# Smaller places for raw weights, a tile of their own for Strassen sums, later squares, and eight more Strassen steps in a hybrid decoder block

## The chip, the core and the metric

The kernel runs on one core of one Trainium2 chip. The metric is the device time of one execution in microseconds (us). TensorE multiplies; VectorE (DVE), ScalarE (ACT) and GpSimd (POOL) do the rest; SyncE (SP), ScalarE and GpSimd issue DMAs. Tiles in on-chip memory have 128 partitions; sizes below are bytes per partition unless they are called MB or belong to a DMA.

## The reference

A decoder block on 256 tokens of 4096 channels, all in float32:

```python
h = rmsnorm(x, norm_w[l])
proj = jnp.einsum('bsd,de->bse', h, w_in[l])
u_p, z_p, u_c, b_c, c_c, z_c, g_logit = jnp.split(proj, SPLIT_POINTS, axis=-1)
y_pool = causal_multiscale_pool(u_p, pool_w[l], pool_scale[l]) * jax.nn.silu(z_p)
y_conv = causal_gated_shortconv(u_c, b_c, c_c, conv_w[l], conv_b[l]) * jax.nn.silu(z_c)
ys = jnp.stack([y_pool, y_conv], axis=2)
br = jnp.einsum('bsnc,ncd->bsnd', ys, w_branch[l])
gates = jax.nn.sigmoid(g_logit.reshape(b, s, N_BRANCHES, d) + gate_b[l])
merged = jnp.sum(gates * br, axis=2)
x = x + jnp.einsum('bsd,de->bse', merged, w_out[l])
...
return rmsnorm(x, final_norm_w)
```

Nearly all of the work is in the three matrix products: w_in (4096 x 20480), w_branch (two of 2048 x 4096) and w_out (4096 x 4096).

## The kernel before, in words

**Units and steps.** The output columns are cut into units of 1024. A unit is a list of steps; a step takes 256 rows of the weight matrix, which is a block of 256 x 1024 or 1 MB, loaded as a raw tile of four quarters of 128 x 512 (2 KB each). The units come in the order cz0 cb0 cu0 cc0 cz1 cb1 cu1 cc1 (convolution branch), pz0 pu0 pz1 pu1 (pooling branch), g0_0 to g1_0 (eight gate units), b0_0 to b1_3 (eight branch units of 8 steps) and o0 to o3 (output); all but the branch units have 16 steps of weights. The text of a unit ("PSPSS...", lines 36 to 49) says of what kind each step is. pz1 and g0_0 also hold a step B (the pooling bands) and two steps M (the 512 x 512 maps of the pooling branch).

**A P step** is the plain product: two halves of rows, two of columns, two of tokens. Each float32 operand is split into a rounded part ("high") and the remainder ("low"), and three products high x high, high x low, low x high are summed, so a P step has 2 x 2 x 2 x 3 = 24 matmuls of 128 x 128 by 128 x 512. **An S step** does the same block by Strassen's scheme with seven products in place of eight: 7 x 3 = 21 matmuls. For that it needs sums of weight quarters as well as quarters (`formed` and `plain`), and sums of activations, which stand in the arena or, for activations kept for P steps, in a small `side` tile that a DMA fills.

**Preparing a step.** `highs` (line 241) rounds quarters into cells of the ring with ScalarE; `lows` (line 245) writes raw minus rounded into other cells with VectorE. The ring (line 209) has 26 cells of 2 KB. They are handed out in order, a block only when all of its cells are free; TensorE frees the two cells of a quarter after the products with it. A P step takes 4 + 4 cells. An S step takes blocks of 3, 3, 4 and 4: the rounded first three quarters, their remainders (`whole`), the two outer sums with their remainders (`outer`), the two inner ones (`inner`), in this order. The sums are made in place in the raw tile. The fourth quarter of an S step is first loaded as it is, and then a gather of POOL adds the third quarter to it in memory.

**What sets the order.** The program is written out by one pass over the units. After each product group (`after_group`) the work list is pumped (`pump`, line 1015): a raw load is issued when the step that had its place before is prepared, and the next piece of preparation is issued when it belongs to a step at most four ahead (AHEAD) and its block of cells is free. After every six matmuls (TICK) one entry of a queue is issued, in which the epilogue of the unit before lies: the entry None passes a tick. So each engine has a fixed order of instructions, and an engine that waits keeps back all that stands behind it: ScalarE's roundings, evacuations and squares, VectorE's sums and remainders, POOL's gathers (raw corners, the corner products J added to E, the residual rows), SP's raw loads.

**Places.** `raw` has five places of 8 KB (NRAW). `issue_load` (line 999) loads a P step with one DMA of 1 MB and an S step with one of 256 KB, one of 768 KB and the gather. Place i serves the loads i, i + 5, i + 10 and so on, and is free when the whole step is prepared.

**The epilogue of an output unit** (`out_unit`, line 767) runs during the next unit: POOL adds the corner products J to E with two gathers, then two row gathers add the residual x to E, ScalarE squares the two rows with a running sum (`square`), VectorE multiplies by the final weight, and E is stored to o_d. In the last unit, o3, the residual of the last 1024 columns is loaded into a free raw place (`rest = slot(0)`, line 1195), and the stored rows of the other three units come back into raw places (`unpark`, line 1178), before the final scaling.

Of the kernel before, what the change touches and what calls it, by code (L numbers as in the profile page):

```python
# [15 lines left out]
P = 128  # L16
# [11 lines left out]
NRAW = 5  # L28
# [12 lines left out]
NINE_P = "PSPSSPSPSSPSSPSP"  # L41
# [10 lines left out]
def hybrid_block(ctx: ExitStack, tc: tile.TileContext, x, xc, prm, rows_in, w_in, pool_w, w_branch, w_out, out):  # L52
# [56 lines left out]
    raw = sb("raw", [P, NRAW, 2 * NU])  # L109
# [145 lines left out]
    class Step:  # L255
        def __init__(self, unit, kind, src=None, op=None, **kw):
            self.unit, self.kind, self.src, self.op = unit, kind, src, op
            self.__dict__.update(kw)
            self.raw = None
            self.prepared = self.halved = False  # L260
            self.pre, self.mid = [], []

        def first(self):
# [3 lines left out]
            def rounded(cells):  # L267
                self.q = self.raw.rearrange("p (i c) -> p i c", i=4)
                self.cells = cells
                if self in steps[:2]:  # L270
                    for i in range(4):
                        if self is steps[0] and i == 0:
                            copy(ring[:, cells[0]], self.q[:, 0])
                        else:
                            highs(cells[i:i + 1], self.q[:, i:i + 1])
                elif self.halved:
                    for i in (0, 2):
                        highs(cells[i:i + 2], self.q[:, i:i + 2])
                else:
                    highs(cells, self.q[:, 0:len(cells)])  # L280

            return [(3 if self.kind == "S" else 4, None, rounded)]

        def rest(self):
            if self.kind == "P":
                def rests(to):
                    self.lows = to
                    if self in steps[:2]:
                        for i in range(4):
                            if self is steps[0] and i % 2 == 0:  # L290
                                x_low(0, 1 - i // 2)
                            lows(to[i:i + 1], self.cells[i:i + 1], self.q[:, i:i + 1])
                    elif self.halved:
                        for i in (0, 2):
                            lows(to[i:i + 2], self.cells[i:i + 2], self.q[:, i:i + 2])
                    else:
                        lows(to, self.cells, self.q)

                return [(4, None, rests)] + self.mid
            if self.kind == "S":  # L300
# [975 lines left out]
```

## Time and profile before

| | us |
|---|---|
| median of the runs shown (3) | 2388.03 (2387.68 to 2392.0) |
| the profiled execution, own time | 2385.66 |
| its span, first to last instruction | 2383.9 |
| TensorE busy | 2346.6 (98%) |
| VectorE busy | 2138.2 (90%) |
| ScalarE busy | 1488.3 (62%) |
| POOL busy | 287.0 (12%) |
| mean granted TensorE clock | 0.995 of full speed |

A profile is of one execution. Busy time is the time in which an engine worked on something; idle time in brackets behind an instruction is that of its engine just before it, with what ended it. TensorE's busy time says nothing of its speed, so the number of matmuls in a stretch of known length is counted beside it. Names such as "ring<-raw" give the tile written and the tile read. L62 is the helper for sums and remainders on VectorE, L59 that for roundings, squares and copies on ScalarE, L89 the gather on POOL and L1054 the matmul.

### The profile page before, as it was taken

To read this page: it belongs to the slowest core of one execution; us is meant where nothing else is said; L and a number is where in the kernel's file an instruction comes from. 1 tells how busy PE (TensorE), PEld (TensorE's weight loads), DVE (VectorE), ACT (ScalarE), POOL (GpSimd) and SP (SyncE) were. 2 spreads that over 40 slices of the span, in tenths; PEclk is the share of its full clock that TensorE was granted. 3 is DMA by queue.
4 is the path that set the end of the run, shared out by engine and by line. 5 is a ranking of instruction groups with operands and counts; after the bars stand their busy time and mean duration, and the time that the engine had idled before them with its cause. 6 is when DMAs were issued, how large, how long until landed. Compare 5 with 4: busy or idle time off the path is not lost.

```text
span 2383.9 us, 28821 instructions
## 1 busy us (share of the span) xinstructions
PE 2346.6 (98%) x10424; PEld 1938.5 (81%) x10424; DVE 2138.2 (90%) x2208; ACT 1488.3 (62%) x1565; POOL 287.0 (12%) x342
## 2 busy tenths in 40 slices
PE   9999999999999999999999999999999999999997
PEld 7888888888888888888888888888878887887785
DVE  8799988999979979979999999988998888998887
ACT  6665655756656656656766666665756656556564
POOL 0001100111001201201111111110000100011110
PEclk9999999999999999999999999999999999999998
DMA  9789876988868768868999999999978888887996
GB/s 385 242 254 282 251 239 213 282 258 252 262 221 247 265 197 253 262 199 253 283 284 282 284 303 285 283 281 298 272 226 282 252 281 281 255 256 237 288 271 230
DMA packets 167711, 627.70 MB, mean 263 GB/s; under 512 B 17424, under 2 KB 25872, under 8 KB 135568
## 3 DMA queue, kind: packets, MB, share of 16 engines
q1 hardware_dynamic: 101792, 485.40, 56.9%
q0 software_dynamic: 48128, 98.59, 23.3%
q10 hardware_dynamic: 17648, 41.87, 5.0%
q8 instruction: 81, 1.33, 0.2%
q14 instruction: 62, 0.51, 0.1%
HBM read 579.66 MB, written 25.17 MB: 254 GB/s over the span
## 4 chain that ended last, share of the span: by engine, by line
PE 89%; DMA 4%; DVE 3%; issue 2%; ACT 1%; POOL 0%; SPq 0%; DVEq 0%; ACTq 0%; POOLq 0%
PE sums L1054 64%; PE shared L1054 23%; DVE ring L62 2%; DMA raw<-in_w_out_dram 1%; PE shared L696 1%; DMA E<-in_x_dram 1%; DMA raw<-in_w_branch_dram 1%; PE shared L482 1%; ACT ring L59 1%; DMA E<-J 1%; DMA raw<-in_w_in_dram 1%; DMA raw<-in_x_dram 0%; DVE E L62 0%; DVE raw L62 0%; POOL E L89 0%
## 5 line engine op out<-in xcount | busy, mean ns | idle before, releaser
L59 ACT ACTIVATE ring<-raw 128x1024 fp32r<-128x1024 f32 (+3 forms) x1089 | 1226.1, 1171 | 748.5 <-DVE raw L62 555.2
L1054 PE MATMUL sums<-ring,arena 128*128 128x512 f32 x7011 | 1642.5, 390 | 13.5 <-DVE ring L62 11.1
L62 DVE TENSOR_TENSOR ring<-raw,ring 128x1024 fp32r<-128x1024 f32 (+2 forms) x1338 | 1467.2, 1141 | 147.8 <-ACT ring L59 73.8
L1054 PEld LDWEIGHTS sums<-ring,arena 128*128 128x128 f32 x7011 | 1313.5, 188 | 290.4 <-DVE ring L62 15.5
L1054 PE MATMUL shared<-ring,arena 128*128 128x512 f32 x2241 | 545.8, 391 | 7.6 <-ACT ring L59 5.5
L1054 PEld LDWEIGHTS shared<-ring,arena 128*128 128x128 f32 x2241 | 422.3, 189 | 98.0 <-ACT ring L59 6.3
L62 DVE TENSOR_TENSOR raw<-raw 128x512 f32<-128x512 f32 (+1 forms) x444 | 424.4, 956 | 10.0 <-DMA raw<-in_w_out_dram 2.3
L89 POOL DMA_DIRECT2D raw<-in_w_in_dram x168 | 145.5, 866 | 1362.9 <-DMA raw<-in_w_in_dram 572.1
L62 DVE TENSOR_TENSOR J<-J 128x512 f32<-128x512 f32 (+1 forms) x90 | 78.2, 869 | 14.7 <-ACT J L59 12.5
L1054 PE MATMUL sums<-ring,last_pair 128*128 128x512 f32 x306 | 76.2, 389 | 0.0
L59 ACT ACTIVATE J<-shared 128x512 f32<-128x512 f32 x128 | 69.9, 601 | 4.2 <-PE shared L482 2.9
L1054 PEld LDWEIGHTS sums<-ring,last_pair 128*128 128x128 f32 x306 | 57.4, 188 | 11.9
L59 ACT ACTIVATE E<-sums 128x512 f32<-128x512 f32 x76 | 41.8, 598 | 28.4 <-PE sums L1054 27.6
L89 POOL DMA_DIRECT2D raw<-in_w_out_dram x31 | 28.0, 904 | 258.5 <-DMA raw<-in_w_out_dram 85.5
L89 POOL DMA_DIRECT2D raw<-in_w_branch_dram x23 | 20.0, 869 | 302.4 <-DMA raw<-in_w_branch_dram 142.2
L1054 PE MATMUL shared<-ring,last_pair 128*128 128x512 f32 x216 | 51.9, 389 | 0.0
L1054 PE MATMUL shared<-ring,side 128*128 128x512 f32 x207 | 50.7, 389 | 0.0
L1054 PEld LDWEIGHTS shared<-ring,last_pair 128*128 128x128 f32 x216 | 40.6, 188 | 8.4
L1054 PEld LDWEIGHTS shared<-ring,side 128*128 128x128 f32 x207 | 38.9, 188 | 8.1
L89 POOL DMA_DIRECT2D E<-J x28 | 38.9, 1469 | 13.4 <-ACT ring L59 13.4
L62 DVE TENSOR_TENSOR E<-E,Y 128x2048 f32<-128x2048 f32 x9 | 20.6, 2287 | 7.2 <-ACT Y L59 7.1
L59 ACT ACTIVATE E<-E 128x1024 f32<-128x1024 f32 x16 | 16.7, 1048 | 11.6 <-DMA E<-in_x_dram 11.6
(120 smaller groups left out, 594.7 us busy)
## 6 DMA issues: line engine op xcount, KB each, us to landing
raw<-in_w_in_dram SPq DMA_DIRECT2D x150, 1024.0 KB, 7.2
raw<-in_w_in_dram SPq DMA_DIRECT2D x168, 768.0 KB, 6.8
raw<-in_w_in_dram SPq DMA_DIRECT2D x176, 256.0 KB, 5.1
raw<-in_w_in_dram POOLq DMA_DIRECT2D x168, 256.0 KB, 6.7
raw<-in_w_branch_dram SPq DMA_DIRECT2D x41, 1024.0 KB, 7.5
raw<-in_w_out_dram SPq DMA_DIRECT2D x33, 1024.0 KB, 6.9
raw<-in_w_out_dram SPq DMA_DIRECT2D x31, 768.0 KB, 7.1
raw<-in_w_branch_dram SPq DMA_DIRECT2D x23, 768.0 KB, 6.9
```

Of the source, the lines that this page charges most:

```text
L59: return pin(nc.scalar.activation(dst, src, func, **kw))
L62: return pin(nc.vector.tensor_tensor(out=dst, in0=a, in1=b, op=op))
L89: return pin(nc.gpsimd.dma_start(dst, src, accum_op=ALU.add))
L482: pin(nc.tensor.transpose(shared(j)[:, i * T + t * P:i * T + (t + 1) * P], src[:, t, c:c + P], ident))
L696: pin(nc.tensor.matmul(o, a, b, start=(k, i) == (0, 0), stop=(k, i) == (3, 2)))
L1054: pin(nc.tensor.matmul(ps, lhs, rhs, start=n == 0, stop=n == u.total[b] - 1))
```

## The change

Five things are changed together.

1. `raw` has four places of 6 KB for the first three quarters and five of 2 KB for the fourth, the corner. Corners have their own issue (`issue_corner`), one step further ahead than the rest; a corner's place is free once it was used (`summed`), a place of 6 KB when the step is prepared. A P step's raw data now comes with two DMAs, and it is rounded and split in pieces of three quarters and one.
2. The sums of an S step go to a tile `parts` of 6 KB. The step's blocks are 4 (rounded, the corner too), 4 (remainders: the corner's at once) and 6 (three sums and their remainders). The remainders of the raw quarters are written in the last piece, `split`. The corner is used as it is now, before it was one of the outer sums.
3. Eight P steps become S steps, one in each of cu0, cu1, cc0, cc1, pu0 and pu1, which go from nine S steps to ten, and one in each of cz1 and pz0, which go from six to seven; the texts of these two now hold S steps in pairs. A unit of ten S steps uses the side tile for two different operands, so each of the six gets a `side_load` on POOL, behind its first S step.
4. In the output units the row gathers come three ticks later and the squares five.
5. The residual in o3 goes to J, and the stored rows come back into the twelve blocks of the places of 6 KB.

The core of the diff:

```diff
-NRAW = 5
+NRAW = 4
+NSUM = 5
...
-NINE_P = "PSPSSPSPSSPSSPSP"
+TEN_P = "PSPSSPSSPSSPSSSP"
+SEVEN5 = "PPPPPSPSSPSPSSPS"
...
-    raw = sb("raw", [P, NRAW, 2 * NU])
+    raw = sb("raw", [P, 3 * NRAW + NSUM, NH])
+    parts = sb("parts", [P, 3, NH])
...
+                elif self.kind == "S":
+                    highs(cells[3:4], self.corner)
+                    highs(cells[0:3], self.raw)
...
-                def whole(to):
-                    self.lows = to
-                    c, q = self.cells, self.q
-                    lows(to[1:2], c[1:2], q[:, 1:2])
-                    lows([to[0], to[2]], [c[0], c[2]], q[:, 0:3:2])
-
-                def outer(cells):
-                    q = self.q
-                    self.outer = cells
-                    sub(q[:, 1], q[:, 3], q[:, 1])
-                    sub(q[:, 0:3:2], q[:, 0:3:2], q[:, 1:2].to_broadcast([P, 2, NH]))
-                    highs(cells[0:2], q[:, 1:4:2])
-                    lows(cells[2:4], cells[0:2], q[:, 1:4:2])
...
-                return [(3, None, whole)] + self.mid + [(4, None, outer), (4, None, inner)]
+                def added(to):
+                    q, w, d = self.raw, self.corner, self.cells
+                    self.lows = to
+                    sub(parts[:, 0], w[:, 0], q[:, 1])
+                    lows(to[3:4], d[3:4], w)
+                    sub(parts[:, 1:3], q[:, 0:3:2], parts[:, 0:1].to_broadcast([P, 2, NH]))
+                    self.summed = True
+
+                def split(cells):
+                    self.sum_cells, self.sum_lows = cells[0:3], cells[3:6]
+                    highs(cells[0:1], parts[:, 0:1])
+                    highs(cells[1:3], parts[:, 1:3])
+                    lows(self.lows[0:3], self.cells[0:3], self.raw)
+                    lows(cells[3:6], cells[0:3], parts)
+
+                return [(4, None, added)] + self.mid + [(6, None, split)]
...
-                         "N5": (Q5, formed(3), ("F", 0, 1)),
+                         "N5": (Q5, plain(3), ("F", 0, 1)),
...
-            return gap(3) + [lambda: row(0), None, lambda: row(1)] + gap(3) + [start] + gap(9) + [
+            return gap(6) + [lambda: row(0), None, lambda: row(1)] + gap(3) + [start] + gap(11) + [
...
+    def issue_corner(s):
+        i = s.load_index
+        c = 3 * NRAW + i % NSUM
+        r = raw[:, c]
+        load(r, s.src[:, 3 * NH:])
+        if s.kind == "S":
+            gather(r, s.src[:, 2 * NH:3 * NH])
+        s.corner = raw[:, c:c + 1]
...
+            nc_ = state["corners"]
+            ahead = EARLY if nc_ < 16 else NSUM
+            if 2 <= nc_ < len(loaded) and (nc_ < ahead or loaded[nc_ - ahead].summed):
+                issue_corner(loaded[nc_])
+                state["corners"] += 1
+                moved = True
...
-            rest = slot(0)
+            rest = J.rearrange("p (t n) c -> p t (n c)", t=2)
```

How VectorE's instructions move is seen in cz1, behind the second group of taps of the convolution (the tile Y): there stood a P step and an S step, and stand a P and an S step. Before, a P step's remainders are the pair ahead of `ring 128x512`; then come whole, the two sums in place (raw<-raw), and outer, inner and the next P step as one run:

```order
L74 SCALAR_TENSOR_TENSOR Y<-E,par,Y 128x254 x2
L62 TENSOR_TENSOR ring<-raw,ring 128x1024 x2
L62 TENSOR_TENSOR ring<-raw,ring 128x512
L62 TENSOR_TENSOR ring<-raw,ring 128x2x512
L62 TENSOR_TENSOR raw<-raw 128x512
L62 TENSOR_TENSOR raw<-raw 128x2x512
L62 TENSOR_TENSOR ring<-raw,ring 128x1024 x4
```

Now, at the taps ahead of it:

```order
L76 SCALAR_TENSOR_TENSOR Y<-E,par,Y 128x254 x2
L64 TENSOR_TENSOR parts<-raw 128x512
L64 TENSOR_TENSOR ring<-raw,ring 128x512
L64 TENSOR_TENSOR parts<-raw,parts 128x1024
L64 TENSOR_TENSOR ring<-raw,ring 128x1536
L64 TENSOR_TENSOR ring<-parts,ring 128x1536
L64 TENSOR_TENSOR ring<-raw,ring 128x1536
L64 TENSOR_TENSOR ring<-raw,ring 128x512
```

The taps of the second group (the four SCALAR_TENSOR_TENSORs) now stand right ahead of the second S step of a pair. Its first three lines are sum, corner remainder and two sums; only the fourth line holds the remainders of the raw quarters, which were the first to be written before. The last two lines are the P step behind it.

How ScalarE's instructions move is seen in o1, around the squares of o0's rows (Y,ossq<-E). Before:

```order
L83 DMA Y<-in_rows_dram 128x1024
L59 ACTIVATE ring<-raw 128x1024 x2
L59 ACTIVATE ring<-raw 128x1536
L83 DMA sa<-m_d 128x512
L59 ACTIVATE ring<-raw 128x1024 x2
L59 ACTIVATE ring<-raw 128x1536
L59 ACTIVATE Y,ossq<-E 128x1024 x2
L59 ACTIVATE ring<-raw 128x1024 x4
L59 ACTIVATE ring<-raw 128x1536
```

Now:

```order
L61 ACTIVATE ring<-parts 128x512
L61 ACTIVATE ring<-parts 128x1024
L61 ACTIVATE ring<-raw 128x1536
L61 ACTIVATE ring<-raw 128x512
L61 ACTIVATE Y,ossq<-E 128x1024
L61 ACTIVATE ring<-raw 128x512
L61 ACTIVATE ring<-raw 128x1536
L61 ACTIVATE Y,ossq<-E 128x1024
L61 ACTIVATE side<-sa 128x512
```

The squares stand about one and a half steps further back, behind the roundings of both S steps of the pair in o1, and one S step's roundings, corner first, now stand between the two of them.

More of the change, by code (lines that the diff above doesn't have):

```diff
@@ L285, in rest @@
             if self.kind == "P":
[L286 removed]
+                return [(4, None, self.rests)] + self.mid
+            if self.kind == "S":
+                def added(to):
+                    q, w, d = self.raw, self.corner, self.cells
                     self.lows = to
[L288 to L297, printed above, removed]
```

82 lines of the change are left out of this document (38 added, 44 removed).

## The prediction

> **What bounds the kernel now.** The page comes first: its span, and the busy time of the engines.
>
> ```profile
> span 2383.9 us, 28821 instructions
> PE 2346.6 (98%) x10424; PEld 1938.5 (81%) x10424; DVE 2138.2 (90%) x2208; ACT 1488.3 (62%) x1565; POOL 287.0 (12%) x342
> ```
>
> TensorE is busy for 98% of the span, so time can go in two ways only: fewer matmuls, or fewer of the gaps between them. One matmul is priced by the chain that ended last, in a stretch without a gap (start, duration, what).
>
> ```profile
> 1282.21 7.48 PE sums L1054 x33
> ```
>
> 7.48 / 33 = 0.2267 us each. The gaps show when the span is cut into stretches of 20 us (columns: stretch, length, then busy time and count of PE, PEld, DVE, ACT, POOL, then granted clock, DMA share, GB/s). An undisturbed stretch counts 90 matmuls, as in the first row; the other rows are all the places with a loss of over ten, except the first and the last 24 us.
>
> ```profile
> 1300.00:1320.00 20.00, 20.00 (x90) 16.57 (x89) 19.44 (x21) 13.64 (x14) 5.20 (x6) 1.00 1.03 320
> ...
> 1740.00:1760.00 20.00, 17.63 (x77) 13.92 (x76) 18.16 (x20) 14.22 (x17) 0.00 (x0) 1.00 0.51 171
> ...
> 2000.00:2020.00 20.00, 16.98 (x75) 13.76 (x74) 16.89 (x14) 11.59 (x11) 0.00 (x0) 1.00 0.88 317
> ...
> 2140.00:2160.00 20.00, 14.76 (x56) 10.93 (x54) 9.74 (x10) 9.06 (x11) 2.60 (x3) 0.85 0.79 219
> ...
> 2240.00:2260.00 20.00, 16.53 (x71) 12.79 (x70) 17.36 (x16) 11.75 (x12) 2.54 (x3) 1.00 0.91 282
> ...
> 2320.00:2340.00 20.00, 17.94 (x72) 14.32 (x72) 12.84 (x13) 9.07 (x10) 0.86 (x1) 0.91 0.85 261
> ```
>
> The last three lie in the output units o1, o2 and o3, one each, and lost 34, 19 and 18 matmuls: 71 x 0.2267 = 16.1 us. The two before them lie in the branch units and lost 13 and 15, which is 6.3 us. The order of time in o1 says why (start, duration, engine, what, and in brackets the idle time before it with its releaser).
>
> ```profile
> 2127.87 1.55 POOL L89 DMA_DIRECT2D E<-J  x1
> ...
> 2142.54 0.86 POOL L89 DMA_DIRECT2D E<-in_x_dram  x1 [11.22 <-DMA E<-J]
> 2149.05 1.06 ACT L59 ACTIVATE Y<-E 128x1024 f32<-128x1024 f32 x1 [7.45 <-DMA E<-in_x_dram]
> 2153.36 1.06 ACT L59 ACTIVATE Y<-E 128x1024 f32<-128x1024 f32 x1 [3.17 <-DMA E<-in_x_dram]
> 2155.51 0.79 PE L1054 MATMUL shared<-ring,arena 128*128 128x512 f32 x1 [4.46 <-ACT ring L59]
> ```
>
> ScalarE reaches the first square at 2149.05 - 7.45 = 2141.6 and stands there until the residual row has been added to E by a gather; that gather stood behind the J gathers. ScalarE's roundings for the ring stand behind the squares, and TensorE behind these. The other two units repeat it.
>
> ```profile
> 2236.53 1.06 ACT L59 ACTIVATE Y<-E 128x1024 f32<-128x1024 f32 x1 [5.83 <-DMA E<-in_x_dram]
> ...
> 2320.05 1.06 ACT L59 ACTIVATE Y<-E 128x1024 f32<-128x1024 f32 x1 [3.54 <-DMA E<-in_x_dram]
> ...
> 2325.87 1.06 ACT L59 ACTIVATE Y<-E 128x1024 f32<-128x1024 f32 x1 [4.67 <-DMA E<-in_x_dram]
> ```
>
> **The change part by part.** The sum starts from the profiled execution's own 2385.66 us, its span of 2383.9 and 1.76 around it. The three runs shown have a median of 2388.03, 2.37 more, which is added at the end.
>
> *Eight Strassen steps.* A P step issues 24 matmuls and an S step 21, so eight exchanges remove 24 x 0.2267 = 5.4 us, if the other engines keep up in the units that get them. The whole-unit stretches, in the same columns: cu0 with nine S steps, and a gate unit that already has ten.
>
> ```profile
> 172.50:253.50 81.00, 81.00 (x359) 67.11 (x358) 75.45 (x75) 49.07 (x51) 11.04 (x12) 1.00 0.89 273
> ...
> 1269.00:1349.30 80.30, 80.30 (x356) 66.53 (x355) 76.39 (x78) 54.51 (x57) 13.49 (x15) 1.00 0.97 290
> ```
>
> The gate unit runs without a gap with VectorE at 76.4 of 80.3 us. What an S step costs VectorE comes from the groups kept apart by shape (busy, mean ns, idle before).
>
> ```profile
> L62 DVE TENSOR_TENSOR ring<-raw,ring 128x1024 fp32r<-128x1024 f32 x980 | 1170.0, 1222 | 89.3 <-PE sums L1054 48.9 <-ACT ring L59 35.6 <-ACT Y L59 1.0
> ...
> L62 DVE TENSOR_TENSOR raw<-raw 128x1024 f32<-128x1024 f32 x222 | 272.1, 1226 | 7.7
> L62 DVE TENSOR_TENSOR ring<-raw,ring 128x512 fp32r<-128x512 f32 x306 | 203.6, 686 | 38.5 <-ACT ring L59 22.2 <-PE sums L1054 8.0 <-ACT E L59 3.4
> ```
>
> From 512 to 1024 elements the time grows by 0.54, so 1536 is an estimate of 1.76. Before, S is one cell, a pair, two sums and two pairs: 0.69 + 1.22 + 0.69 + 1.23 + 1.22 + 1.22 = 6.27 us. Now it is sum, cell, sum, three, three: 0.69 + 0.69 + 1.23 + 1.76 + 1.76 = 6.13. P is 2.44 either way. cu0 thus ends near 75.45 + (6.13 - 2.44) - 9 x 0.14 = 77.9 of 80.2 us: fuller than the gate unit, not over. The six more side loads and eight more gathers are issued by POOL, which is idle for 66.8 us of the gate unit; I cost them at nothing. If that cover were gone, a gather would delay its S step by its landing, 6.7 us:
>
> ```profile
> raw<-in_w_in_dram POOLq DMA_DIRECT2D x168, 256.0 KB, 6.7
> ```
>
> *The new order inside an S step.* This is where cost can hide, because the ring has 26 cells and S takes 14 of them. Take P, S, S, in this order. While the first S and the head of the second hold 18 cells, the remaining 8 are P's. The second S's block for remainders can be had when P is through, 21 matmuls or 4.76 us before the second S starts. Then follow corner remainder, second sum and the three raw remainders, and only these let its first product run. How soon VectorE moves after such a release, two rows show: the S step's shared products begin six matmuls (1.36 us) into it, so it began at 2133.88, and VectorE at 2134.16.
>
> ```profile
> 2134.16 3.03 DVE L62 TENSOR_TENSOR ring<-raw,ring 128x1024 fp32r<-128x1024 f32 x4 [1.51 <-PE sums L1054]
> ...
> 2135.24 2.88 PE L1054 MATMUL shared<-ring,arena 128*128 128x512 f32 x12
> ```
>
> 0.28 + 0.69 + 1.23 + 1.76 = 3.96 us, against 4.76 and one more matmul, 4.99: about 1.0 us is left. Before, the block bound at that point was the outer sums, which are needed by the fourth product only: 0.28 + 0.69 + 1.23 + 1.22 = 3.4 against 4.99 + 2.04, 3.6 us left. So 75 steps that follow an S keep 1.0 us of 3.6. In the plain cycle S, S, P VectorE needs 2 x 6.13 + 2.44 = 14.7 of 14.96 us even unoverlapped, so lag does not build up and I cost this at nothing there. Where VectorE has other work right ahead of a second S, it does cost. The second taps of a z unit lie there now:
>
> ```profile
> 378.36 1.76 DVE L74 SCALAR_TENSOR_TENSOR Y<-E,par,Y 128x255 f32<-128x255 f32 x4 [1.16 <-ACT Y L59]
> ```
>
> They take 1.16 + 1.76 = 2.9, less the 1.0 left and the 0.3 to spare in a cycle: 1.6 us each in cz1 and pz0. In the branch units four late places, each deeper by up to the 0.7 that P loses (its first remainders now come in a group of 1.76 and not of 1.22, and the corner after it), give 2. I put +5 on all of this, between 0 and 75 x 0.3 = 22.
>
> *Four places of 6 KB and five of 2 KB.* A raw load now leaves four steps ahead, not five, in two pieces for P too.
>
> ```profile
> raw<-in_w_in_dram SPq DMA_DIRECT2D x150, 1024.0 KB, 7.2
> raw<-in_w_in_dram SPq DMA_DIRECT2D x168, 768.0 KB, 6.8
> raw<-in_w_in_dram SPq DMA_DIRECT2D x176, 256.0 KB, 5.1
> ```
>
> The least room is behind a first S. Its block of six can be had 24 matmuls (5.4 us) before it starts, with P's start, so VectorE is through 0.28 + 1.76 + 1.76 later, 1.6 us before the start, and the load lands at +5.2. The step four further on is a second S, which starts at 3 x 4.76 + 5.44 = +19.7. Its four cells for rounding are free when the step two ahead of it begins, 24 + 21 = 45 matmuls earlier (26 - 14 - 8 = 4), at +9.5. That leaves 4.3 us over the median landing, about one step less than before. I cost it at 0, with the rows as bounds: 6.8 in place of 7.2 would be a gain, 5.1 + 6.8 one after the other 11.9, which is 0.8 past the margin. The Trainium skill speaks against the split: "DMA: Bandwidth & Descriptors", section Rules for kernel authors, asks for at least 1 MiB per DMA for the best bandwidth. By it the two pieces would end later than the whole; the three rows have 5.1 and 6.8 against 7.2, and none shows the pieces of one P together.
>
> *Later squares.* They move by five ticks of six matmuls, 30 x 0.2267 = 6.8 us; the row gathers by three, which matters little, since in o1 the first was late by POOL's queue and the second by E<-J anyway. Then the first square is reached at 2141.6 + 6.8 = 2148.4 and waits 0.7 of 7.45; the second, two ticks later, waits some 2.2 of 3.17. o2 and o3 wait next to nothing. VectorE's product behind the squares moves with them and stays under the ring's lead; bare, it costs its 2.29 (the shape of the first row below). In o2 and o3 a raw gather now stands between the two row gathers on POOL: at nothing, since the second row waits longer for E<-J (11.22 above) than a corner for its landing. Gained: 16.1, less 3 for what remains of o1 and for the corner, which is now rounded ahead of the raw cells and so can meet a late gather in the same place: -13, between -10 and -16. Counting waits alone, PE's missing busy time in the three rows is 5.24 + 3.47 + 2.06 = 10.8; the rest went with clocks of 0.85 and 0.91. "TensorE: Matmul & The Clock Gate", Part 1, in the Trainium skill has the clock halved after an idle window of about 3.4 us; by the Trainium skill the 2.06 would cost itself alone, and the 16.1 would be 14.1. The row with 0.91 disagrees.
>
> *The tail.* The residual for the last columns goes to J.
>
> ```profile
> 2362.67 2.29 DVE L62 TENSOR_TENSOR E<-E,raw 128x2048 f32<-128x2048 f32 x1 [3.50 <-DMA raw<-in_x_dram]
> 2365.07 0.69 DVE L62 TENSOR_TENSOR E<-sums,E 128x512 f32<-128x512 f32 x1
> ...
> 2371.27 0.68 DVE L62 TENSOR_TENSOR E<-sums,E 128x512 f32<-128x512 f32 x1
> ```
>
> Its DMA is issued at the same place of ScalarE's queue, but the three parked loads now wait for the last preparations, so it shares less. VectorE waited 3.50 for it; I take half of what can come through, -1.5, between 0 and -3.5. Next late is then the parked rows.
>
> Sum: 2385.66 - 5.4 + 5 - 13 - 1.5 = 2370.8, and + 2.37 gives 2373 us.
>
> **The rivals.** *The second S of a pair waits for VectorE (slower).* Place: the first product of the 75 steps. It decides once VectorE is over 1.0 us late at the release. For it: VectorE's 97% in cu0. Against: the gate unit's 3.9 us of idle VectorE. At 1.0 + 0.3 us late everywhere it costs 22, not 5: 2390; at 0.5 beyond, 38: 2406. Taken at 2397.
>
> *The wait in the output units only moves.* The gathered corner is needed at the rounding, 45 matmuls ahead, and not at the outer sums. For it: the gather issued behind J's waits just as the rows do. Against: nothing due stands behind that rounding for 6 us. The 13 are lost: 2386.
>
> *The loads come late.* A landing on the chain in o1 took this long:
>
> ```profile
> 2117.07 9.51 DMA raw<-in_w_out_dram
> ```
>
> The median of the larger pieces there is 7.1.
>
> ```profile
> raw<-in_w_out_dram SPq DMA_DIRECT2D x31, 768.0 KB, 7.1
> ```
>
> Two pieces end to end (11.9) and these 2.4 more are 3.2 past the margin of 11.1; less the 1.0 left, once in each of the thirteen units of ten S steps, 29: 2402. The Trainium skill's rule on the size of a DMA (above) would show in this way.
>
> *More goes than counted.* If the branch gaps (6.3) and my +5 vanish too: 2362.
>
> **How the numbers follow.** The forecast, with its own range 2364 to 2383, has 0.63; the first rival 0.12, the second 0.14, the third 0.04, the last 0.07. A difference of 0.2% (4.8 us) is about what the measurement can tell. Below 2383.2: 0.61 of the forecast, the 0.07, and 0.05 of the second rival: 0.73. Within 0.2%: 0.02 + 0.09 + 0.03 of the first: 0.14. Slower: 0.13. The range 2363 to 2389 leaves out about half of the last rival and nearly all of the first and third: 0.19.
>
> **What would show it.** Right: PE at 24 matmuls fewer, 88 to 90 per 20 us through o1 to o3 with clock 1.00; squares idle under 4 us in sum, not 24.7; no idle of PE behind "DVE ring" in the gate units. Wrong: "PEld sums <- DVE ring" with dozens of waits; ScalarE's 128x512 rounding behind a raw DMA for many microseconds; VectorE over 78 us in a gate unit.

## The result, and the profile after

| | before | after |
|---|---|---|
| median of the runs, us | 2387.86 (4 runs) | 2363.84 (2362.52 to 2364.46, 4 runs) |
| ratio, 95% interval | | 0.9896 [0.9879, 0.9913] |
| the profiled execution, own time | 2385.66 | 2364.46 |
| its span | 2383.9 | 2362.7 |

The kernel became 24.0 us faster; 15 were forecast. In the changed kernel the helpers have moved by a few lines: VectorE's sums and remainders are L64, ScalarE's roundings and squares L61, the gather L91, the matmul L1062. The page, span and engines:

```profile
span 2362.7 us, 29641 instructions
PE 2342.9 (99%) x10400; PEld 1931.7 (82%) x10400; DVE 2115.2 (90%) x2126; ACT 1528.7 (65%) x1896; POOL 293.8 (12%) x356
```

TensorE has the 24 matmuls fewer that were announced, but its busy time fell by only 3.7 us, and the span by 21.2. Most of the gain lies in gaps. The stretches of 20 us that lie in o1, o2 and o3 (columns as in the prediction):

```profile
2120.00:2140.00 20.00, 20.00 (x90) 16.56 (x89) 17.26 (x15) 12.01 (x14) 5.29 (x6) 1.00 1.03 291
2140.00:2160.00 20.00, 20.00 (x89) 16.52 (x88) 18.34 (x21) 13.67 (x18) 2.12 (x3) 1.00 1.00 320
...
2240.00:2260.00 20.00, 20.00 (x90) 16.53 (x90) 18.93 (x19) 11.45 (x14) 1.72 (x2) 1.00 0.92 279
2320.00:2340.00 20.00, 20.00 (x90) 16.55 (x89) 18.93 (x19) 12.40 (x15) 0.00 (x0) 1.00 0.67 250
```

They count 89 or 90 matmuls at full clock where 56, 71 and 72 stood. The order of time on ScalarE in o1 has the two squares without idle ahead of them, and no other square of this trace waits for a residual row either, where 24.7 us were waited before:

```profile
2145.23 1.99 ACT L61 ACTIVATE ring<-raw 128x1536 fp32r<-128x1536 f32 x2
2147.12 1.04 ACT L61 ACTIVATE Y<-E 128x1024 f32<-128x1024 f32 x1
...
2150.06 1.04 ACT L61 ACTIVATE Y<-E 128x1024 f32<-128x1024 f32 x1
```

Where the rest came from, and went, is not seen in slices. A finer measure is the length of each unit, from the start of one unit's first evacuation to the start of the next one's. The rows for a gate unit, of the kernel before and of the changed one:

```profile
1348.21 0.60 ACT L59 ACTIVATE E<-sums 128x512 f32<-128x512 f32 x1 [1.30 <-PE sums L1054]
...
1428.45 0.60 ACT L59 ACTIVATE E<-sums 128x512 f32<-128x512 f32 x1 [1.37 <-PE sums L1054]
```

```profile
1351.22 0.60 ACT L61 ACTIVATE E<-sums 128x512 f32<-128x512 f32 x1 [1.99 <-PE sums L1062]
...
1431.72 0.60 ACT L61 ACTIVATE E<-sums 128x512 f32<-128x512 f32 x1 [2.07 <-PE sums L1062]
```

80.24 us before, 80.50 after, though this unit's text is the same in both. Such a length repeats within 0.02 us from gate unit to gate unit. The whole span cut in this way, after minus before:

| stretch | forecast | measured |
|---|---|---|
| start to the seventh gate unit | -2.2 (-5.4 and 3.2 for the z units) | +3.8 |
| the last gate unit, the branch units and o0 | +1.8 | -6.5 |
| o1, o2 and o3 up to TensorE's last matmul | -13 | -15.3 |
| from there to the end | -1.5 | -3.2 |

So by the seventh gate unit the changed kernel was behind, and all of its gain comes later. What TensorE's queue of weight loads waited for says where it lost. The view of waits, before and after (who, for whom, us in total, times, longest):

```profile
PEld sums L1054 <- DVE ring L62: 15.5, 11, 3.4
PE sums L1054 <- DVE ring L62: 11.1, 8, 3.0
```

```profile
PEld sums L1062 <- DVE ring L64: 17.8, 32, 1.5
PE sums L1062 <- DVE ring L64: 5.7, 11, 1.1
```

A few long waits became many short ones: 32 in place of 11. In the gate unit above there is one, and VectorE's rows ahead of it name its cause:

```profile
1274.87 0.69 DVE L64 TENSOR_TENSOR ring<-raw,ring 128x512 fp32r<-128x512 f32 x1 [2.49 <-PE shared L1062]
1275.48 1.22 DVE L64 TENSOR_TENSOR parts<-raw,parts 128x1024 f32<-128x1024 f32 x1
1276.66 2.68 DVE L64 TENSOR_TENSOR J<-J 128x512 f32<-128x512 f32 x3
1279.25 1.75 DVE L64 TENSOR_TENSOR ring<-raw,ring 128x1536 fp32r<-128x1536 f32 x1
```

```profile
1281.06 0.30 PEld L1062 LDWEIGHTS sums<-ring,arena 128*128 128x128 f32 x2 [0.37 <-DVE ring L64]
```

(These are of the gate unit before it, where the same stands.) The step that waits is the first S step of the unit, behind its first P step; its first product needs the remainders of the raw quarters, and these end at 1281.0. Ahead of them stand the three sums of the corner products J of the unit before, 2.68 us: they fell between the step's two pieces, `added` and `split`. Of the 32 waits 16 stand at this place, 10.3 us into a unit. TensorE's busy time does not show this at all; it was 78.00 of 78.00 us in both kernels. "Perfetto Trace Analysis" in the Trainium skill, section Identifying the Most-Contended Engine, says that matmul busy time is no good measure of how near TensorE is to its limit, and names the busy time of weight loads as one of two to use instead; this trace agrees, with 64.29 us of weight loads in those 78 against 64.61 before.

### The profile page after: what moved, and what is told of

The parts are those of the page before. It is cut to its first block, busy times and chain, and to the rows that moved or that the text cites. A ratio compares the mean times of both kernels' runs of the same rounds, so it can differ in the third digit from the quotient of the medians.

```text
span 2362.7 us, 29641 instructions
## 1 busy us (share of the span) xinstructions
PE 2342.9 (99%) x10400; PEld 1931.7 (82%) x10400; DVE 2115.2 (90%) x2126; ACT 1528.7 (65%) x1896; POOL 293.8 (12%) x356
## 4 chain that ended last, share of the span: by engine, by line
PE 91%; DVE 5%; issue 1%; DMA 1%; ACT 1%; POOL 0%; DVEq 0%; SPq 0%; ACTq 0%; POOLq 0%
PE sums L1062 65%; PE shared L1062 24%; DVE ring L64 3%; DVE parts L64 1%; PE shared L691 1%; PE shared L477 1%; DMA raw<-in_w_in_dram 1%; ACT ring L61 1%; DMA J<-in_x_dram 0%; DVE E L64 0%; DVE Y L76 0%; DVE J L64 0%; PE shared L667 0%; DVE Y L64 0%; DVE raw L1224 0%
## 5 line engine op out<-in xcount | busy, mean ns | idle before, releaser
L1062 PE MATMUL sums<-ring,arena 128*128 128x512 f32 x6873 | 1616.6, 390 | 5.1 <-DVE ring L64 4.2
L1062 PEld LDWEIGHTS sums<-ring,arena 128*128 128x128 f32 x6873 | 1287.2, 188 | 281.2 <-DVE ring L64 14.4
L64 DVE TENSOR_TENSOR ring<-raw,ring 128x1536 fp32r<-128x1536 f32 (+2 forms) x978 | 1088.1, 1138 | 151.1 <-PE shared L1062 49.3
L61 ACT ACTIVATE ring<-raw 128x512 fp32r<-128x512 f32 (+1 forms) x943 | 899.9, 1014 | 107.8 <-PE sums L1062 82.0
L61 ACT ACTIVATE ring<-parts 128x1024 fp32r<-128x1024 f32 (+1 forms) x477 | 389.6, 828 | 545.2 <-DVE parts L64 505.3
L1062 PE MATMUL shared<-ring,arena 128*128 128x512 f32 x2283 | 552.1, 389 | 0.0
L1062 PEld LDWEIGHTS shared<-ring,arena 128*128 128x128 f32 x2283 | 428.5, 188 | 89.4
L64 DVE TENSOR_TENSOR ring<-parts,ring 128x1536 fp32r<-128x1536 f32 (+2 forms) x262 | 405.1, 1556 | 15.0 <-PE sums L1062 7.7
L91 POOL DMA_DIRECT2D raw<-in_w_in_dram x176 | 152.2, 865 | 1377.7 <-DMA raw<-in_w_in_dram 554.8
L64 DVE TENSOR_TENSOR parts<-raw,parts 128x1024 f32<-128x1024 f32 x230 | 280.3, 1219 | 0.0
L64 DVE TENSOR_TENSOR parts<-raw 128x512 f32<-128x512 f32 x230 | 157.7, 685 | 2.1
L64 DVE TENSOR_TENSOR J<-J 128x512 f32<-128x512 f32 (+1 forms) x90 | 78.2, 869 | 15.7 <-ACT J L61 13.2
L1062 PE MATMUL sums<-ring,last_pair 128*128 128x512 f32 x306 | 77.4, 391 | 1.7 <-DVE ring L64 1.5
L61 ACT ACTIVATE J<-shared 128x512 f32<-128x512 f32 x128 | 68.1, 620 | 8.5 <-PE shared L477 4.4
L61 ACT ACTIVATE E<-sums 128x512 f32<-128x512 f32 x76 | 42.2, 598 | 45.8 <-PE sums L1062 44.9
L1062 PEld LDWEIGHTS sums<-ring,last_pair 128*128 128x128 f32 x306 | 57.1, 188 | 15.2 <-DVE ring L64 3.4
L1062 PE MATMUL shared<-ring,side 128*128 128x512 f32 x261 | 63.9, 389 | 0.0
L91 POOL DMA_DIRECT2D raw<-in_w_out_dram x31 | 27.0, 871 | 269.7 <-DMA raw<-in_w_out_dram 118.0
L1062 PEld LDWEIGHTS shared<-ring,side 128*128 128x128 f32 x261 | 49.0, 188 | 10.3
L91 POOL DMA_DIRECT2D raw<-in_w_branch_dram x23 | 20.0, 868 | 295.2 <-DMA raw<-in_w_branch_dram 150.1
L1062 PE MATMUL shared<-ring,last_pair 128*128 128x512 f32 x216 | 51.9, 389 | 0.0
L1062 PEld LDWEIGHTS shared<-ring,last_pair 128*128 128x128 f32 x216 | 40.5, 188 | 8.4
```

Of the source, the lines that this page charges most:

```text
L61: return pin(nc.scalar.activation(dst, src, func, **kw))
L64: return pin(nc.vector.tensor_tensor(out=dst, in0=a, in1=b, op=op))
L91: return pin(nc.gpsimd.dma_start(dst, src, accum_op=ALU.add))
L1062: pin(nc.tensor.matmul(ps, lhs, rhs, start=n == 0, stop=n == u.total[b] - 1))
```

## The experiments

The kernel before had medians of 2382.89 to 2387.86 on the chips of these runs, so a few us are compared within one chip, or by the lengths of units. The lengths are of one execution each, and pu0 and pu1 are the least steady: pu0 took 83.89 and 85.32 us in two kernels below that differ in the last unit alone.

**Does the order inside an S step cost the time?** Three edits build on each other. The first writes the raw remainders with the sums:

```diff
                     sub(parts[:, 1:3], q[:, 0:3:2], parts[:, 0:1].to_broadcast([P, 2, NH]))
+                    lows(to[0:3], d[0:3], q)
                     self.summed = True
...
-                    lows(self.lows[0:3], self.cells[0:3], self.raw)
```

> Only VectorE's order changes: the remainders of the three raw quarters are written in the piece that makes the sums, not in the one behind it. At 24 places other work (mostly the three sums of the corner products J, 2.7 us) stood between the two. Theory order: the 0.26 us that each unit of ten S steps lost is that work, standing ahead of the second S step's first product; nine such units, the output units and one or two branch units win 0.25 to 0.4 us each, about 3.5 in all: 2360.3 us, between 2359 and 2362. Theory load: VectorE has too much work in these units, whatever its order: 2363.8, no change.

2359.35 us (2358.03 to 2360.52). The theory of the order holds, though the S step that waited is the unit's first and not its second. VectorE at the same place of the same gate unit:

```profile
1274.04 1.22 DVE L64 TENSOR_TENSOR parts<-raw,parts 128x1024 f32<-128x1024 f32 x1
1275.17 1.75 DVE L64 TENSOR_TENSOR ring<-raw,ring 128x1536 fp32r<-128x1536 f32 x1
1276.84 2.67 DVE L64 TENSOR_TENSOR J<-J 128x512 f32<-128x512 f32 x3
```

J's sums now stand behind the remainders, which end 7.6 us into the unit and not 10.3; each gate unit is back at 80.24.

The second edit also puts the corner's remainder behind those of the raw quarters:

```diff
                     sub(parts[:, 0], w[:, 0], q[:, 1])
-                    lows(to[3:4], d[3:4], w)
                     sub(parts[:, 1:3], q[:, 0:3:2], parts[:, 0:1].to_broadcast([P, 2, NH]))
                     lows(to[0:3], d[0:3], q)
+                    lows(to[3:4], d[3:4], w)
```

> As the kernel with early remainders, and the corner's remainder, 0.69 us, is written behind those of the raw quarters and not ahead of them, so the second S step's first product has 1.7 us of slack and not 1.0. Theory order: the three waits in pu0 and the two in pu1 (together 4.4 us) lose up to 0.69 each, so 2 to 3 us go on top of the 3.5: 2357.5 us, between 2356.5 and 2360. Theory load: in pu0 with three S steps in a row VectorE is behind by its work alone and only the place of the wait moves: as the kernel with early remainders, or 1 us slower because the corner's remainder is now late for the fourth product.

2357.80 us (2355.55 to 2358.47), as forecast, but not by the items forecast. In the traces pz0 fell by 2.2 and cz1 by 0.8; pu0 by 1.1 and pu1 by 2.6, of which an unknown part is chance; and the last unit grew from 98.85 to 101.15. In it VectorE now stood for the residual:

```profile
2332.73 2.29 DVE L64 TENSOR_TENSOR E<-E,J 128x2048 f32<-128x2048 f32 x1 [4.46 <-DMA J<-in_x_dram]
```

The third edit loads the residual three steps earlier, where J has long been free:

```diff
         if st is lead[-4]:
             flush()
+            rest = J.rearrange("p (t n) c -> p t (n c)", t=2)
+            move(rest, xrows[:, :, 3 * NU:])
             last.before()
...
-            rest = J.rearrange("p (t n) c -> p t (n c)", t=2)
-            move(rest, xrows[:, :, 3 * NU:])
             corners(E)
```

> As the kernel with the corner's remainder behind the raw ones, and the residual of the last columns is loaded into J before o3's ninth S step's end, three steps earlier on ScalarE's queue than before. There VectorE waited 4.46 us for it ahead of the last sums. Theory landing: the wait goes and the last unit falls from 101.15 to some 96.7 us: total 2353.4, between 2351.5 and 2355. Theory next: what is late next, the stored rows that come back, takes its place within 1 or 2 us: 2356 to 2357.

2354.13 us (2353.22 to 2355.50). The wait for the residual is gone and the last unit is 98.13, not the 96.7 expected. VectorE's first sum of the tail is now released by TensorE, so nothing else is late next:

```profile
2333.35 0.69 DVE L64 TENSOR_TENSOR E<-sums,E 128x512 f32<-128x512 f32 x1 [0.84 <-PE sums L1062]
```

**What are the eight Strassen steps worth?** First in the changed kernel: the texts of the kernel before, with all else as changed.

```diff
-TEN_P = "PSPSSPSSPSSPSSSP"
+NINE_P = "PSPSSPSPSSPSSPSP"
...
-                    FIRST if first else SEVEN5, dst=Y)
+                    FIRST if first else SIX5, dst=Y)
...
-        u = in_unit(f"cu{c}", base, lambda u: rescale(Y), TEN, dst=Y)
+        u = in_unit(f"cu{c}", base, lambda u: rescale(Y), NINE, dst=Y)
...
-        in_unit(f"cc{c}", base + 2 * HALF, c_epi, TEN).urgent = lambda: mul(E, E, Y)
+        in_unit(f"cc{c}", base + 2 * HALF, c_epi, NINE_A).urgent = lambda: mul(E, E, Y)
...
-            if u.text in (TEN, TEN_P) and st is next(q for q in u.main if q.kind == "S"):
+            if u.text is TEN and st is next(q for q in u.main if q.kind == "S"):
```

> The changed kernel with the old texts: the eight Strassen steps are plain again, all else is as changed. Theory eaten: the eight exchanges cost about 7.4 us of new waits in their own units (pu0 3.0, pz0 1.6, pu1 1.4, the rest 1.4) against 5.4 us of matmuls saved, so without them the kernel is 2 us faster: 2362, between 2360.5 and 2363.5. Theory saved: each exchange is worth its 0.68 us and the loss has other causes: 2369.3.

2362.80 us (2362.09 to 2363.91), span 2361.1 against 2362.7. In the changed kernel the eight exchanges are worth nothing: what they save in cu0 to cc1 they lose in pu0 and pz0, by the lengths of units. Then the same texts in the kernel with the early residual:

> As the kernel with early residual, and the eight Strassen steps plain again. Theory order: with the remainders early the eight exchanges lose nothing any more but in pu0 (some 1.5 to 2.5 us), so taking them back costs 3 to 4.5 us: 2358, between 2356.5 and 2359.5; cu0, cc0, cu1 and cc1 go from 80.24 to 80.92 each. Theory load: a unit with ten S steps is at VectorE's limit, the exchanges are worth nothing, and the time stays at 2354.

2356.87 us (2356.37 to 2357.92). With the order mended the exchanges are worth what the matmuls say, 0.68 us in each of cu0, cc0, cu1 and cc1 (80.24 against 80.92).

In pu0 the new text has three S steps in a row. In the changed kernel its weight loads waited at the second and the third (the last two of these rows; the first lies beside POOL's masks):

```profile
805.41 1.01 PEld L1062 LDWEIGHTS sums<-ring,arena 128*128 128x128 f32 x5 [0.84 <-DVE ring L64]
820.83 0.99 PEld L1062 LDWEIGHTS sums<-ring,last_pair 128*128 128x128 f32 x5 [0.54 <-DVE ring L64]
826.63 0.30 PEld L1062 LDWEIGHTS sums<-ring,arena 128*128 128x128 f32 x2 [1.17 <-DVE ring L64]
```

Three S steps need 3 x 6.1 us of VectorE in 3 x 4.76 of TensorE. No order tried inside the step mends that: the third of the row waited between 1.06 and 1.30 us in all nine traces with this text. So the ten are put in pairs, on top of the early residual:

```diff
-TEN_P = "PSPSSPSSPSSPSSSP"
+TEN_P = "PSSPSSPSSPSSPSSP"
```

> As the kernel with early residual, and the text of pu0 and pu1 has its ten S steps in five pairs, none in a row of three. Theory triple: the two weight loads that waited 1.15 and 1.30 us at the second and third S of the row in pu0 wait under 0.3; pu0 falls from 85.3 (83.9 in another run) to 82.5 to 83.2, pu1 from 88.3 to 87.7: 2351.5, between 2350 and 2353.5. Theory masks: what counts in pu0 is VectorE's wait for POOL's masks (1.4 to 2.8 us), which stays: 2354, and pu0 over 83.8.

2351.88 us (2351.03 to 2352.12), ratio 0.9864 [0.9844, 0.9883] to the kernel before: the fastest of all. pu0 is 83.38, a little over the range, pu1 87.72. The waits at the place of the row of three are gone. What that is worth is less sure: the kernel with the early residual ran on another chip, where its ratio was 0.9867, and pu0 was 83.89 without pairs in the trace before that, so it is between 0.5 and 1.9 us in pu0. Nearly all the waits for VectorE's cells that are left:

```profile
PEld sums L1062 <- DVE ring L64: 2.6, 5, 0.8
...
PE sums L1062 <- DVE ring L64: 0.7, 2, 0.4
```

On the same chip the changed kernel was run again as the measure.

> The changed kernel once more, on the same chip as the other runs of this call, as their measure: 2363.8, between 2361 and 2365; every unit within 0.3 us of its first trace except pu0 and pu1, where VectorE waits for masks that POOL makes between two gathers, within 1.5.

2363.87 us (2363.36 to 2365.27); the units repeat within 0.3. So the three small edits and the pairs are worth 12.0 us on top of the change, and the eight exchanges 2356.87 - 2351.88 = 5.0 of their 5.4. Lengths of some units, us:

| unit | before | after | remainders early | corner behind | residual early | pairs |
|---|---|---|---|---|---|---|
| cu0 | 80.92 | 80.58 | 80.42 | 80.24 | 80.24 | 80.24 |
| pz0 | 87.55 | 88.47 | 88.45 | 86.23 | 86.21 | 86.20 |
| pu0 | 83.13 | 85.44 | 84.97 | 83.89 | 85.32 | 83.38 |
| pu1 | 88.40 | 89.13 | 90.44 | 87.88 | 88.26 | 87.72 |
| fifth gate unit | 80.24 | 80.50 | 80.24 | 80.24 | 80.24 | 80.24 |
| b7 (b1_3) | 47.29 | 45.02 | 44.21 | 44.22 | 44.20 | 44.23 |
| o3 to the end | 106.03 | 99.11 | 98.85 | 101.15 | 98.13 | 98.09 |

**Is it the later squares that mended the output units?** Their ticks alone, in the kernel before, and the other way round in the changed one:

```diff
-            return gap(3) + [lambda: row(0), None, lambda: row(1)] + gap(3) + [start] + gap(9) + [
+            return gap(6) + [lambda: row(0), None, lambda: row(1)] + gap(3) + [start] + gap(11) + [
```

> The kernel before with one edit: row gathers three ticks and squares five ticks later in the output units. Theory squares, as predicted: the waits of the squares shrink from 24.7 us to about 4 and the output units win 10 to 16 us: 2373, between 2370 and 2376; o1 goes from 89.5 to some 83. Theory both suffice: the same here, since the new order of corners and sums and the later squares each take away the same waits. Theory order: the ring's blocks and the corner's place are what counts, and the old order still stalls: at most 6 us, 2380.

2370.91 us (2367.21 to 2373.92), 14.7 below the kernel before on the same chip. o1, o2 and o3 together, to the end of the span, fell from 279.99 to 263.01, by 17.0. (Two branch units took 3.9 us longer in this trace, behind a product of VectorE that waited 6.60 us for a landing.) So the edit does by itself what was forecast for it, and a little more.

> The changed kernel with the row gathers and squares of the output units at their old ticks. Theory squares: nearly all that the output units won (8.3 in o1, 3.3 in o2, some 3 in o3) is owed to the later ticks: 2378, between 2374 and 2381. Theory order: the new place of corner and gathers on POOL already took half of the waits away: 2369 to 2373.

2369.97 us (2366.03 to 2371.14): the first theory falls, and the time lies in the range of the second. The profiled execution is the fastest of the five. In its trace o1 and o2 lose 2.4 us to the old ticks, not 11.6, and the squares wait 7.3 us in all; by the medians the old ticks cost 6.1 us, and no trace shows where the rest of that lies.

```profile
ACT Y L61 <- DMA E<-in_x_dram: 7.3, 4, 3.5
```

Something else in the change had taken these waits away as well. A corner has a fifth place, which is free early; POOL's gather for it stands between the gathers of J and of the rows. So, with the old squares:

```diff
-NSUM = 5
+NSUM = 4
```

> The changed kernel with the squares at their old ticks and four places for corners, not five, so that a corner is loaded and gathered one step later. Theory corner: with old squares o1 is 83.3 us and not the 89.5 of before because the corner's gather, which stands on POOL between the two gathers of J, starts some 5 us earlier; one step less gives most of that back: o1 86 to 90, the second gather of J over 21 us behind the end of the unit and not 19.1, total 2375 to 2380. Theory blocks: the gather of J and the corner are not what counts, but that ScalarE no longer stands behind sums made in place: o1 stays at 83.3, total 2370.

2385.66 us (2383.16 to 2388.57): all of the change's gain is gone. The theory of the corner holds, and more strongly than it said; but the second gather of J, which it had expected over 21 us behind the unit's end, was issued some 12 us behind it. What waited, on ScalarE, was the corner's rounding:

```profile
2143.70 0.63 ACT L61 ACTIVATE ring<-raw 128x512 fp32r<-128x512 f32 x1 [7.44 <-DMA raw<-in_w_out_dram]
...
2153.66 2.00 ACT L61 ACTIVATE ring<-raw 128x512 fp32r<-128x512 f32 x2 [6.31 <-DMA raw<-in_w_out_dram]
2155.57 1.04 ACT L61 ACTIVATE Y<-E 128x1024 f32<-128x1024 f32 x1
```

The squares themselves no longer wait for the residual rows. Then four places with the later squares, to see whether that rounding cares for them:

> The changed kernel, later squares and all, with four places for corners and not five. With four places and old squares o1 took 91.85 and o2 87.00 us, and ScalarE stood not at the squares but at the corner's rounding, 7.44 and 6.31 us behind a late gather. Theory corner: that rounding does not care where the squares stand, so o1 stays over 87 and o2 over 84: 2378 to 2385. Theory squares: with the squares out of the way the gathers come earlier or ScalarE catches up, and o1 is at 83 or less: 2368 to 2373.

2368.37 us (2367.11 to 2371.20); the theory of the corner falls here. ScalarE still waits for corners, but for less:

```profile
2139.58 0.63 ACT L61 ACTIVATE ring<-raw 128x512 fp32r<-128x512 f32 x1 [6.08 <-DMA raw<-in_w_out_dram]
2146.82 2.01 ACT L61 ACTIVATE ring<-raw 128x512 fp32r<-128x512 f32 x2 [3.58 <-DMA raw<-in_w_out_dram]
```

POOL's rows tell the difference. With the old ticks both rows are gathered and then the corner; with the later ones the corner's gather comes between them.

```profile
2136.32 2.00 POOL L91 DMA_DIRECT2D E<-in_x_dram  x2
2138.27 0.95 POOL L91 DMA_DIRECT2D raw<-in_w_out_dram  x1
```

```profile
2132.22 1.11 POOL L91 DMA_DIRECT2D E<-in_x_dram  x1
2135.39 0.86 POOL L91 DMA_DIRECT2D raw<-in_w_out_dram  x1 [2.06 <-DMA raw<-in_w_out_dram]
2135.94 1.22 POOL L91 DMA_DIRECT2D E<-in_x_dram  x1
```

Behind two rows the corner was there after 2153.66 - 2138.27 = 15.4 us, behind one after 2146.82 - 2135.39 = 11.4. o1 and o2 together, in one trace of each of the six cases:

| | old ticks | later ticks |
|---|---|---|
| kernel before (five places of 8 KB) | 173.96 | 162.62 |
| changed, four places for corners | 178.85 | 164.72 |
| changed, five places for corners | 164.76 | 162.39 |

In these traces either of the two takes most of the loss away; without both it is worse than before. One edit's worth read in the presence of the other is 2.3 or 2.4 us, in its absence 14.1. The medians of the whole kernel say the same less sharply: the later ticks are worth 6.1 us with five places for corners and 17.3 with four, the fifth place 4.5 us with the later ticks and 15.7 with the old ones. So neither edit makes the other quite superfluous.

**How near are the loads to being late?** Three places of 6 KB in place of four:

```diff
-NRAW = 4
+NRAW = 3
```

> The changed kernel with three places of 6 KB for raw quarters in place of four: a load of 768 KB leaves one step later, 4.76 to 5.44 us. Theory margin, as the prediction worked it out: four places leave 4.3 us over the median landing at the tightest step, so three are 0.5 to 1.1 us short there and several us short for a slow landing; ScalarE's roundings wait for raw in every unit of ten S steps: 13 to 40 us, 2377 to 2404. Theory room: preparation runs further behind its limits than reckoned, the margin is larger than a step, and nothing happens: 2364 to 2368.

2370.48 us (2368.48 to 2372.47): between the two, nearer to the theory of room. The waits of the changed kernel for raw data, and those with three places:

```profile
ACT ring L61 <- DMA raw<-in_w_in_dram: 7.7, 8, 1.8
...
ACT ring L61 <- DMA raw<-in_w_out_dram: 3.2, 1, 3.2
```

```profile
ACT ring L61 <- DMA raw<-in_w_in_dram: 66.8, 56, 4.1
...
ACT ring L61 <- DMA raw<-in_w_branch_dram: 36.3, 22, 4.4
ACT ring L61 <- DMA raw<-in_w_out_dram: 30.1, 15, 5.3
...
PE sums L1062 <- DVE ring L64: 9.7, 16, 1.5
```

ScalarE waits for loads 93 times, 133 us in all. TensorE's waits for VectorE's cells grow by 4.0 us (from 5.7), those of its weight loads by 6.7 (from 17.8 to 24.5), and the span by 5.1. A load that comes late for a rounding is not yet late for a product.

## Why the prediction was right, and where not

The forecast of 2373 was 9 us too high: 6.3 by its sum (2370.8 against 2364.46), and the rest because 2.37 was added for the median, where the profiled execution of the changed kernel lies 0.6 above its median. That the sum is as near as that is luck: up to the seventh gate unit the kernel lost 6.0 us against the forecast, and in the branches it won 8.3. Of the signs of being wrong one came, dozens of waits of weight loads for VectorE.

**Eight Strassen steps, -5.4.** The term is right (5.0 once nothing hides it), and it was lost again on the way. The step that failed is the one on the plain cycle: "lag does not build up and I cost this at nothing there", with other work named only in the z units and the branches. It looked at S steps that follow an S alone, and found 1.0 us of slack there. Half of the waits stand at a unit's first S step, which follows a P. J's sums are written out when the unit before closes, and that is between the two pieces of this step: 2.68 us, against some 2.3 that it had to spare by the rows above (an estimate), or 0.25 us in each of nine units with ten S steps. The three S steps in a row in pu0 were not costed at all: 3.0 us there with VectorE's other work, against the 0.7 saved. The z units' 1.6 each came as 1.6 in pz0 and as 0.6 behind cz1, but not by the item that was priced. In cz1 the taps stand right ahead of a second S step, at 376.45, and no weight load waited behind them; the 0.6 lies in cb1, at the place of J's sums. In pz0 one weight load waited 0.67 us behind taps, and the longest wait, 1.52, is that of a P step, behind a product of the epilogue (E<-J,Y, 2.28 us). The first rival had the right mechanism, VectorE late for an S step's first product, but half of the waits stand at another place than its own; its price of 22 us took all 75 steps to be late at once, where 32 weight loads waited, 17.8 us in all.

**The branches, +1.8.** They won 5.8 with the last gate unit, and o0 0.7. The step added only costs and left out that waits there could go. The last rival had counted two gaps, 6.3, and one of them went: in b7 VectorE's product of the epilogue had stood 2.92 us for J's gather, with the remainders behind it; after, no such product waits, and b7 won 2.3. Before, two other products waited 4.38 us each, in b3 and b5, which won only 0.2 and 0.1. The waits of before:

```profile
DVE Y L62 <- DMA E<-J: 7.3, 2, 4.4
DVE Y L62 <- DMA raw<-in_w_branch_dram: 4.4, 1, 4.4
```

The other gap, in b1, stayed: b1 took 43.44 us before and 43.57 after. After the change, in the two stretches that the prediction showed:

```profile
1740.00:1760.00 20.00, 18.52 (x81) 14.62 (x80) 19.48 (x22) 14.75 (x18) 0.00 (x0) 1.00 0.56 198
2000.00:2020.00 20.00, 20.00 (x90) 16.57 (x89) 19.83 (x22) 12.44 (x17) 0.00 (x0) 1.00 0.91 325
```

The rest of the gain lies in the eighth gate unit and b0 (2.6 together), where TensorE had waited 1.09 us for an evacuation by ScalarE, and in b6 (0.8). Which part of the change removes these waits was not isolated: for b7 neither the fifth corner place nor the texts do it, since with four places or the old texts b7 is 45.0 as well, and the later squares do not, since with them alone it is 46.9. The new order of S with its tile for sums is what is left of the larger edits, and that it is the cause is argued, not shown.

**Places and loads, 0.** Right: nothing that TensorE needs waits for a load. "DMA: Bandwidth & Descriptors", section Rules for kernel authors, in the Trainium skill wants 1 MiB per DMA; the pieces of a step landed after 7.1 us (768 KB) and 6.0 (256 KB, 5.1 before), against 7.2 for the whole. No cost of that shows here: ScalarE waited 10.9 us for raw data in the whole kernel, after 3.8 before, and TensorE never did. The margin of 4.3 us was too small a figure for what matters: one step less costs 5 to 7 us and not 13 to 40. What the term did not see is that the fifth place for corners is worth 14 us when the squares are early, so it was no neutral exchange of places. (The 14 us are of o1 and o2 in one trace each.)

**Later squares, -13.** Measured -15.3 in the sum, and -16.5 alone in the kernel before, to the same point (the 17.0 above count the tail too). Right as a term; as an explanation of this kernel it is one of two edits that each remove most of the same wait. The second rival, that the wait only moves to the corner's rounding, is real: it is the kernel with four corner places and the old ticks. The step "the row gathers by three, which matters little" fails there, since one row more ahead of the corner's gather made it 4 us later (15.4 against 11.4).

**The tail, -1.5.** TensorE's last matmul ends 15.1 us ahead of the span's end before and 11.9 after: -3.2, within the bounds of 0 and -3.5. The load was waited for 1.90 us, not 3.50, and it was also issued earlier against TensorE's end. What was said to be late next, the stored rows, never was: with the residual early 11.2 us are left, and TensorE itself is waited for.

## What to carry to other kernels

When an engine's work is cut into pieces that other work can fall between, put what the critical engine needs first into the earliest piece that has the room: one moved line took the median from 2363.84 to 2359.35 us, and an exchange of two lines took it to 2357.80, although the last unit lost 2.3 us by it. Slack computed from the cycle holds only where nothing else stands in it; list everything that the queues can put there, the previous unit's closing sums too, and ahead of every kind of step. And two edits in one change can each remove most of the same wait: undo them one at a time and both together, before saying which of them did it.

## What the runs showed of the hardware

- VectorE's sums took longer while POOL made masks: 1.42 us in place of 1.22 and 1.95 in place of 1.75, at the rows

```profile
802.02 1.73 POOL L627 TENSOR_SCALAR_AFFINE_SELECT sa<-sa 128x256 f32<-128x256 f32 x2
802.07 1.42 DVE L64 TENSOR_TENSOR parts<-raw,parts 128x1024 f32<-128x1024 f32 x1
803.41 1.95 DVE L64 TENSOR_TENSOR ring<-raw,ring 128x1536 fp32r<-128x1536 f32 x1
```

  "SBUF — State Buffer", section Who interferes with whom, in the Trainium skill says that a VectorE instruction with two inputs in on-chip memory contends with a POOL instruction that reads it, and calls the ports that they share an exclusive lock. The lengthening agrees in kind; 0.2 us is far less than the 1.73 that the two selects take together, though a span on POOL is rough.
- A weight load's wait of 0.37 us costs 0.26 us of the unit and leaves TensorE's busy time at 100%. Only the wait itself and the unit's length show it.
- In the kernel with four corner places and old ticks, waits of 7.7 us in one stretch cost 47 matmuls, or 10.7 us, at a granted clock of 0.74; with the later ticks 1.07 us cost 7 matmuls, 1.6 us, at a clock of 1.00.

```profile
2150.00:2170.00 20.00, 12.28 (x43) 9.39 (x42) 14.54 (x17) 11.46 (x15) 0.86 (x1) 0.74 0.73 234
```

```profile
2145.15:2165.15 20.00, 18.93 (x83) 15.12 (x82) 18.23 (x21) 13.86 (x18) 2.59 (x3) 1.00 0.92 281
```
